# LayerNorm's mean and mean square in a one-core decoder layer: fp32 products against a column of ones, or fp32r products of split sums against a constant tile

## The chip, the cores and the metric

The kernel runs on one NeuronCore of one Trainium2 chip. The metric is the device time of one execution in microseconds, the median of several runs. A profile is one further execution with the hardware profiler on. All its times count from the first instruction of the span.

## The reference, cut to what matters

One layer for 288 tokens (256 of a prompt, 8 × 4 of a decoding batch), model width 2048, everything in fp32. The change lies in the convolution branch, in the `layernorm` line:

```
h = rmsnorm(x, norm1_g)
proj = h @ w_in + b_in
a, gate, z = proj[..., :D_CONV], proj[..., D_CONV:2 * D_CONV], proj[..., 2 * D_CONV:]
u = a * jax.nn.sigmoid(gate)
c = jax.nn.silu(layernorm(depthwise_causal_conv(u_ext, conv_w, conv_b), ln_g, ln_b))
p = multiscale_pool(z_ext, pos0) @ pool_w * pool_scale
x = x + jnp.concatenate([c, p], axis=-1) @ w_out
x = x + jnp.square(jax.nn.relu(rmsnorm(x, norm2_g) @ w_ff1)) @ w_ff2
return rmsnorm(x, norm_f)
```

`layernorm` takes mean and variance over the 1024 channels of the convolution, per token.

## The kernel before

**Layout.** Channels lie on the 128 partitions, the 288 tokens along the free axis. A product is 128 × 128 weights against 128 × 288 tokens in one PSUM bank. Each fp32 matrix product is made of three fp32r products of split operands, high × high, low × high, high × low. The activations are split once. The weights come from HBM in 512 KB halves (`wr`). ScalarE writes the high part (`whi`, L275); VectorE (`wlo`, L280), GpSimd (L283) or, in a few cases, a DMA that adds writes the low part. Five buffers of each kind circulate, so the cast of a later half waits until TensorE has read the last product from the buffer that it takes over.

**Order of the work.** `gemm` (L311) writes out the products of one pair of banks, in pairs of k tiles, 12 products per k pair and bank, with all weights of a half used before the next half. Its argument `between` names functions that are called at a given k; what they issue stands there on TensorE, and the products of the gemm that follow are issued after it. The rest of the order on each engine comes from a scheduler that goes by priorities (the order of the code; `later` moves code down by a number) and by its own estimates. Each engine works through its queue in order, so an instruction that waits holds up everything behind it.

**The stages around the change.** First the input projection and pooling run in the order of `SEQUENCE` (L45); the last three steps are the pooling products of group 1, convolution pair 7 and the pooling products of group 0 (`pp`, then `dx` on ScalarE at L510, VectorE at L511). Then eight gemms, called g = 0 to 7 here, multiply the pooled half `mixp` (tiles `dx`) with the lower half of `w_out`. While they run, VectorE finishes the depthwise convolution (L457), and LayerNorm's steps are placed between their products:

- `ln_mean` (L551), at k = 4 of g = 5: two fp32 products of the sums of `c` with `ones`, a 128 × 128 tile of 1/1024. Each shows as two records per product in the trace. `sum_c` holds the sum of seven of the eight channel groups, made on GpSimd; the eighth is the second half of `c`'s last tile.
- `ln_sums` (L556), at k = 6 of g = 6: VectorE subtracts the mean (L559), ScalarE squares (L561), VectorE adds (L565, L566). `rsqrt_sums` (L239) brings 288 sums onto 96 partitions × 3 with three small fp32 products (`pt<-ones,q`), ScalarE takes the root (L251) and loads the table for SiLU (L209), VectorE makes the inverse root by one Newton step (L254 to L257) on 96 × 3 numbers.
- `ln_rows` (L570), at k = 2 of g = 7: `spread` (L260) brings the 288 values back as a row on all 128 partitions, with three fp32 products (`pt<-ident,st`).

After the eight gemms comes the loop over `cs`, four tiles of two channel groups. VectorE multiplies by the row (L587), ScalarE applies SiLU twice (L590) and casts the high part (L592), VectorE makes the low part (L593). These tiles (`mx`) are the operands of the next eight gemms, with the upper half of `w_out`; the first two of them are interleaved on TensorE and begin with the first `mx` tile. Behind them follow the two feed-forward products, which take most of the time, and the last norm.

ScalarE's function tables: Sigmoid during the projections; a dummy activation `few` (L209) loads Sqrt right behind the last Sigmoid (L442, L443), and Silu behind the root (L251).

Second norm (L633): it already has the form that the change gives to LayerNorm, with a cast (L637), a subtraction (L638), two fp32r products with a constant tile, a root over 128 × 288 (L643) and `inverse_root` (L232) on 128 × 288.

Of the kernel before, what the change touches and what calls it, by code (L numbers as in the profile page):

```python
# [86 lines left out]
def trunk_kernel(ctx: ExitStack, tc: tile.TileContext, io):  # L87
# [139 lines left out]
    cst = const.tile([P, 32], F32, name="cst")  # L227
# [206 lines left out]
    def conv_pair(i, banks):  # L434
# [7 lines left out]
        if i == N8 - 1:  # L442
            load_table(AF.Sqrt, tg[:, 0:1])  # L443
# [105 lines left out]
    norm = {}  # L549

    def ln_mean():  # L551
        norm["mean"] = ms("pmean")[:, 0, :T]
        mm(norm["mean"], ones, sum_c[:, 0, :], start=True, stop=False)
        return mm(norm["mean"], ones, cs[-1][:, 1, :], start=False, stop=True)

    def ln_sums():  # L556
        ssc = None
        for c in cs:
            nc.vector.tensor_tensor(c, c, norm["mean"][:, None, :].to_broadcast([P, 2, T]), op=ALU.subtract)  # L559
            q = tmpp.tile([P, 2, T], F32, name=nm("q2"), tag="ag" if ssc is None else "ag2", bufs=2)  # L560
            nc.scalar.activation(q, c, AF.Square)  # L561
            if ssc is None:
                ssc = q
            else:
                nc.vector.tensor_tensor(ssc, ssc, q, op=ALU.add)  # L565
        nc.vector.tensor_tensor(ssc[:, 0, :], ssc[:, 0, :], ssc[:, 1, :], op=ALU.add)  # L566
# [18 lines left out]
    for j, c in enumerate(cs):  # L585
        n = tmpp.tile([P, 2, T], F32, name=nm("n"), tag="ag", bufs=2)
        nc.vector.tensor_tensor(n, c, norm["rows"][:, None, :].to_broadcast([P, 2, T]), op=ALU.mult)  # L587
        for m in range(2):
            i = 2 * j + m
            nc.scalar.activation(n[:, m, :], n[:, m, :], AF.Silu, bias=v("ln_b", i), scale=v("ln_g", i))  # L590
        mh, ml = act2("mx")
        nc.scalar.copy(mh, n)  # L592
        nc.vector.tensor_tensor(ml, n, f32(mh), op=ALU.subtract)  # L593
# [185 lines left out]
```

## Time and profile before

| | us |
|---|---|
| median of 3 runs | 1085.36 (1085.34 to 1086.2) |
| the profiled execution, its own time | 1084.97 |
| its span, first to last instruction | 1082.9 |
| TensorE busy in the span | 1071.1 (99%) |
| mean granted TensorE clock | 0.997 |

The profiled execution lies 0.39 us under the median, and 2.1 us of it lie outside the span. Busy time on TensorE counts overlapping products once, so 99% says that there are hardly any gaps, not that nothing could be gained: a product that is not needed is busy as well.

### The profile page before, as it was taken

Reading aid. Unit: us, or ns where it says so; the run is one execution under the profiler, and the core shown is the slowest. Engines: PE = TensorE matmul, PEld = TensorE weight load, DVE = VectorE, ACT = ScalarE, POOL = GpSimd, SP = SyncE. Lnnn points to the kernel's source line nnn. Section 1 sums busy time; section 2 is a strip of 40 time slices with the busy share of each in tenths; the row PEclk is TensorE's granted clock in tenths of the full one; section 3 lists DMA queues with packets and bytes.
Section 4 is the critical chain, followed back from the end, with each engine's and each line's share of the span. In section 5 each row is a group of like instructions: output and inputs, shape, how many; then the busy total and the mean of one; then the engine's idle time right before and its main releaser. Section 6 shows DMA issues by size and latency. Waiting matters only on the chain.

```text
span 1082.9 us, 19574 instructions
## 1 busy us (share of the span) xinstructions
PE 1071.1 (99%) x8198; PEld 1068.5 (99%) x8198; DVE 636.5 (59%) x817; ACT 477.4 (44%) x584; POOL 173.8 (16%) x180
## 2 busy tenths in 40 slices
PE   9999999999999999999999999999999999999996
PEld 8999999999999999999999999999999999999996
DVE  8899999678655544445544444545544445554552
ACT  8654455475544433334443333444433334444441
POOL 0878979512000000000000000000000000000001
PEclk9999999999999999999999999999999999999998
DMA  9896477545555555555555555555555555555522
GB/s 333 281 268 182 137 209 231 172 152 176 173 163 170 174 168 165 175 164 168 175 169 165 174 167 167 174 171 164 172 169 166 173 172 164 171 172 163 172 78 88
DMA packets 58696, 190.71 MB, mean 176 GB/s; under 512 B 6256, under 2 KB 12016, under 8 KB 58608
## 3 DMA queue, kind: packets, MB, share of 16 engines
q1 hardware_dynamic: 56336, 184.09, 53.0%
q0 software_dynamic: 1008, 3.67, 1.8%
q10 hardware_dynamic: 1264, 1.70, 0.5%
q8 instruction: 64, 1.05, 0.4%
q14 instruction: 24, 0.20, 0.1%
HBM read 185.16 MB, written 4.28 MB: 175 GB/s over the span
## 4 chain that ended last, share of the span: by engine, by line
PE 76%; issue 21%; ACT 1%; DMA 1%; DVE 1%; POOL 0%; SPq 0%; POOLq 0%; DVEq 0%
PE ac L306 75%; DMA wr<-in_w 1%; PE pp L306 0%; ACT whi L275 0%; DVE wlo L280 0%; POOL xT L715 0%; ACT n L590 0%; DVE z_all L414 0%; ACT L209 0%; ACT z_all L412 0%; PE pt L306 0%; PE pmean L306 0%; POOLq L765 0%; DVE xT L690 0%; DVE n L587 0%
## 5 line engine op out<-in xcount | busy, mean ns | idle before, releaser
L275 ACT CAST whi<-wr 128x1024 fp32r<-128x1024 f32 (+1 forms) x341 | 355.5, 1043 | 557.5 <-PE ac L306 536.0
L280 DVE TENSOR_TENSOR wlo<-wr,whi 128x1024 fp32r<-128x1024 f32 (+1 forms) x297 | 363.7, 1225 | 348.4 <-ACT whi L275 348.4
L306 PE MATMUL ac<-ax,whi 128*128 128x288 f32 x2048 | 351.1, 292 | 0.0
L306 PE MATMUL ac<-fx,whi 128*128 128x288 f32 x2048 | 350.2, 292 | 0.0
L306 PEld LDWEIGHTS ac<-ax,whi 128*128 128x128 f32 x2048 | 296.0, 187 | 0.0
L306 PEld LDWEIGHTS ac<-fx,whi 128*128 128x128 f32 x2048 | 295.7, 187 | 0.0
L306 PE MATMUL ac<-ax,wlo 128*128 128x288 f32 x1024 | 217.4, 292 | 0.0
L306 PE MATMUL ac<-fx,wlo 128*128 128x288 f32 x1024 | 216.4, 292 | 0.0
L306 PEld LDWEIGHTS ac<-ax,wlo 128*128 128x128 f32 x1024 | 162.6, 187 | 0.0
L306 PEld LDWEIGHTS ac<-fx,wlo 128*128 128x128 f32 x1024 | 162.3, 187 | 0.0
L306 PE MATMUL ac<-hx,whi 128*128 128x288 f32 x768 | 136.2, 293 | 0.7 <-DVE hx L361 0.3
L715 POOL TENSOR_TENSOR xT<-xT,rf 128x288 f32<-128x288 f32 x4 | 3.0, 792 | 800.1 <-ACT rf L719 800.1
L306 PEld LDWEIGHTS ac<-hx,whi 128*128 128x128 f32 x768 | 113.3, 188 | 1.4 <-ACT whi L275 0.9
L283 POOL TENSOR_TENSOR wlo<-wr,whi 128x512 fp32r<-128x512 f32 x74 | 100.6, 1415 | 35.4 <-ACT whi L275 34.4
L457 DVE SCALAR_TENSOR_TENSOR pc<-u_all,vec,pc 128x256 f32<-128x256 f32 x232 | 99.5, 483 | 1.9 <-ACT pc L454 0.7
L306 PE MATMUL ac<-hx,wlo 128*128 128x288 f32 x384 | 86.2, 293 | 0.3 <-DVE wlo L280 0.2
L306 PEld LDWEIGHTS ac<-hx,wlo 128*128 128x128 f32 x384 | 62.7, 188 | 0.7 <-DVE wlo L280 0.7
L306 PE MATMUL ac<-dx,whi 128*128 128x288 f32 x256 | 46.1, 296 | 0.3 <-ACT dx L510 0.3
L306 PE MATMUL ac<-mx,whi 128*128 128x288 f32 x256 | 45.2, 294 | 0.1
L659 DVE SCALAR_TENSOR_TENSOR t<-ac,r 128x576 f32<-128x576 f32 x32 | 24.2, 758 | 25.2 <-PE ac L306 25.2
L306 PEld LDWEIGHTS ac<-dx,whi 128*128 128x128 f32 x256 | 37.9, 188 | 0.7 <-ACT dx L510 0.6
L306 PEld LDWEIGHTS ac<-mx,whi 128*128 128x128 f32 x256 | 37.5, 188 | 0.6 <-ACT mx L592 0.3
(130 smaller groups left out, 515.0 us busy)
## 6 DMA issues: line engine op xcount, KB each, us to landing
wr<-in_w SPq DMA_DIRECT2D x335, 512.0 KB, 3.7
wlo<-in_w POOLq DMA_DIRECT2D x7, 512.0 KB, 8.5
xT<-in_xT SPq DMA_DIRECT2D x7, 288.0 KB, 7.1
out_u_out<-u_all SPq DMA_DIRECT2D x1, 1208.0 KB, 8.9
u_all<-in_hist_c SPq DMA_DIRECT2D x8, 136.0 KB, 5.6
wr<-in_w SPq DMA_DIRECT2D x4, 256.0 KB, 3.5
out_z_out<-z_all SPq DMA_DIRECT2D x1, 668.0 KB, 8.9
z_all<-in_hist_p SPq DMA_DIRECT2D x4, 152.0 KB, 7.7
```

What stands on the lines that cost most here:

```text
L275: nc.scalar.copy(hi, raw)
L280: nc.vector.tensor_tensor(lo, raw, f32(hi), op=ALU.subtract)
L283: nc.gpsimd.tensor_tensor(lo[:, j : j + 2, :], raw[:, j : j + 2, :], f32(hi[:, j : j + 2, :]), op=ALU.subtract)
L306: last = nc.tensor.matmul(*args, **kw)
L457: nc.vector.scalar_tensor_tensor(out=dst, in0=up[:, w : w + SEQ], scalar=cwv[:, w : w + 1], in1=pc, op0=ALU.mult, op1=ALU.add)
L659: nc.vector.scalar_tensor_tensor(out=t, in0=bk[:, :, :T], scalar=0.0, in1=both(rows2[0]), op0=ALU.max, op1=ALU.mult)
L715: eng.tensor_tensor(xk, xk, r[:, None, :].to_broadcast([P, n, T]), op=ALU.mult)
```

## The change

- The sums of `c` are split into high and low parts (tile `hm`, new lines 553 and 554): ScalarE casts, GpSimd or VectorE subtracts. `ln_mean` becomes four fp32r products with `means_c`, a new constant tile of 1/1024 that GpSimd makes at the start.
- In `ln_sums` the sum of squares is cast by ScalarE and subtracted by VectorE (tile `hs`), and two fp32r products with `means_c` put the mean square on all partitions. Root, table load and `inverse_root` follow on 128 × 288 numbers, the last three steps of it in PSUM. `rsqrt_sums` and `spread` are no longer called here, and `ln_rows` with its three products is gone.
- `ln_sums` and the loop over `cs` stand in `later(-LATER)`, at high priority.
- The load of the Sqrt table moves from the last Sigmoid to behind the last pooling products.

```diff
-        if i == N8 - 1:
-            load_table(AF.Sqrt, tg[:, 0:1])
...
+    load_table(AF.Sqrt, f32(mixp[1][0])[:, 0:1])
...
+    hm = actp.tile([P, 4, T], F32R, name="hm", tag="act")
+    for (hi, lo), part, eng in (((1, 0), sum_c[:, 0, :], nc.gpsimd), ((3, 2), cs[-1][:, 1, :], nc.vector)):
+        nc.scalar.copy(hm[:, hi, :], part)
+        eng.tensor_tensor(hm[:, lo, :], part, f32(hm[:, hi, :]), op=ALU.subtract)
+    def products(bank, parts):
+        for j, part in enumerate(parts):
+            last = mm(bank, means_c, part, start=j == 0, stop=j == len(parts) - 1)
+        return last
     def ln_mean():
         norm["mean"] = ms("pmean")[:, 0, :T]
-        mm(norm["mean"], ones, sum_c[:, 0, :], start=True, stop=False)
-        return mm(norm["mean"], ones, cs[-1][:, 1, :], start=False, stop=True)
+        return products(norm["mean"], [hm[:, j, :] for j in (1, 0, 3, 2)])
...
-        norm["sums"] = rsqrt_sums([ssc[:, 0, :]], 1.0 / DC, AF.Silu)
-        return norm["sums"][2]
-    def ln_rows():
-        norm["rows"], last = spread(norm["sums"])
+            hs = actp.tile([P, 4, T], F32R, name="hs", tag="act")
+            hi, lo = hs[:, 1, :], hs[:, 0, :]
+            nc.scalar.copy(hi, ssc[:, 0, :])
+            nc.vector.tensor_tensor(lo, ssc[:, 0, :], f32(hi), op=ALU.subtract)
+            bk, rl = ms("pt"), row("rl")
+            mean, root = bk[:, 0, :T], bk[:, 1, :T]
+            last = products(mean, [hi, lo])
+            nc.scalar.activation(root, mean, AF.Sqrt, bias=eps)
+            load_table(AF.Silu, root[:, 0:1])
+            inverse_root(mean, root, rl, root)
+            norm["rows"] = root
         return last
-    BETWEEN = {5: {4: ln_mean}, 6: {6: ln_sums}, 7: {2: ln_rows}}
+    BETWEEN = {5: {4: ln_mean}, 6: {6: ln_sums}}
...
     for j, c in enumerate(cs):
...
+        with later(-LATER):
```

How the order on the engines moves. In the changed kernel the line numbers from L229 to L441 are larger by 2 (casts stand at L277, low parts at L282), those from L444 to L546 are as before, and those behind the new code are larger by 17 or 18. Buffer numbers are larger by a few.

**Place 1: ScalarE at the end of the pooling products** (`tg` is the last Sigmoid, `dx` the last two pooling results). Before:

```order
L441 ACTIVATE tg_2193<-ac_2088,vec 128x288
L209 ACT_TABLE_LOAD
L209 ACTIVATE few<-tg_2193 128x1
L510 ACTIVATE dx_2040<-pp_2233,vec 128x288
L275 CAST whi_2386<-wr_2379 128x1024
L454 ACTIVATE pc_1717<-u_all,vec 128x256
L510 ACTIVATE dx_2040<-pp_2233,vec 128x288
L275 CAST whi_2445<-wr_2441 128x1024
```

The same place on ScalarE in the changed kernel:

```order
L443 ACTIVATE tg_2195<-ac_2090,vec 128x288
L510 ACTIVATE dx_2042<-pp_2234,vec 128x288
L277 CAST whi_2393<-wr_2386 128x1024
L454 ACTIVATE pc_1719<-u_all,vec 128x256
L510 ACTIVATE dx_2042<-pp_2234,vec 128x288
L209 ACT_TABLE_LOAD
L209 ACTIVATE few<-dx_2042 128x1
L277 CAST whi_2452<-wr_2448 128x1024
```

The load and its dummy activation have moved behind both `dx`.

**Place 2: VectorE from the end of the squares' sum** (q at 128x288 is its last addition) **to the multiplication by the row**. Before:

```order
L566 TENSOR_TENSOR q_2689<-q_2689 128x288
L280 TENSOR_TENSOR wlo_2804<-wr_2797,whi_2803 128x1024
L250 TENSOR_SCALAR st_2708<-pt_2704 96x3
L254 RECIPROCAL st_2708<-st_2708 96x3
L255 TENSOR_TENSOR st_2708<-st_2708 96x3
L256 SCALAR_TENSOR_TENSOR st_2708<-st_2708 96x3
L257 SCALAR_TENSOR_TENSOR st_2708<-st_2708 96x3
L582 TENSOR_TENSOR xT<-xT,ac_2651 128x576
L280 TENSOR_TENSOR wlo_2891<-wr_2886,whi_2890 128x1024
L587 TENSOR_TENSOR n_2808<-c_637,pt_2704 128x576
L587 TENSOR_TENSOR n_2815<-c_721,pt_2704 128x576
```

The same place on VectorE in the changed kernel:

```order
L577 TENSOR_TENSOR q_2698<-q_2698 128x288
L282 TENSOR_TENSOR wlo_2811<-wr_2804,whi_2810 128x1024
L581 TENSOR_TENSOR hs<-q_2698,hs 128x288
L236 RECIPROCAL rl_2717<-pt_2716 128x288
L599 TENSOR_TENSOR xT<-xT,ac_2660 128x576
L282 TENSOR_TENSOR wlo_2898<-wr_2893,whi_2897 128x1024
L237 SCALAR_TENSOR_TENSOR pt_2716<-pt_2716,rl_2717 128x288
L238 SCALAR_TENSOR_TENSOR pt_2716<-pt_2716,rl_2717 128x288
L239 SCALAR_TENSOR_TENSOR pt_2716<-pt_2716,rl_2717 128x288
L282 TENSOR_TENSOR wlo_2902<-wr_2895,whi_2901 128x1024
L605 TENSOR_TENSOR n_2815<-c_639,pt_2716 128x576
L605 TENSOR_TENSOR n_2822<-c_723,pt_2716 128x576
```

The subtraction for `hs` now stands where TensorE's small result was fetched, behind a low part of weights (`wlo_2811`) that itself waits for a cast; one more low part (`wlo_2902`) has come ahead of the first `n`.

**Place 3: ScalarE from the root to the first `mx` tiles.** Before:

```order
L275 CAST whi_2803<-wr_2797 128x1024
L251 ACTIVATE st_2708<-st_2708 96x3
L209 ACT_TABLE_LOAD
L209 ACTIVATE few<-st_2708 96x1
L275 CAST whi_2890<-wr_2886 128x1024
L590 ACTIVATE n_2808<-n_2808,vec 128x288 x2
L275 CAST whi_2894<-wr_2888 128x1024
L590 ACTIVATE n_2815<-n_2815,vec 128x288 x2
L592 CAST mx_2812<-n_2808 128x576
L592 CAST mx_2819<-n_2815 128x576
L275 CAST whi_2961<-wr_2957 128x1024
```

The same place on ScalarE in the changed kernel:

```order
L277 CAST whi_2810<-wr_2804 128x1024
L580 CAST hs<-q_2698 128x288
L585 ACTIVATE pt_2716<-pt_2716,cst 128x288
L209 ACT_TABLE_LOAD
L209 ACTIVATE few<-pt_2716 128x1
L277 CAST whi_2897<-wr_2893 128x1024
L277 CAST whi_2901<-wr_2895 128x1024
L277 CAST whi_2968<-wr_2964 128x1024
L608 ACTIVATE n_2815<-n_2815,vec 128x288 x2
L608 ACTIVATE n_2822<-n_2822,vec 128x288 x2
L610 CAST mx_2819<-n_2815 128x576
L610 CAST mx_2826<-n_2822 128x576
```

Three weight casts now stand ahead of the first SiLU, where there was one; the third, `whi_2968`, takes over the buffer that g = 7 reads to its end (before, its counterpart `whi_2961` stood behind the two `mx` casts). On TensorE the new products stand where the old ones stood; the order of SyncE's and GpSimd's DMAs is unchanged.

More of the change, by code (lines that the diff above doesn't have):

```diff
@@ L226, in trunk_kernel @@
     nc.vector.tensor_scalar(means, ones, DC / D, None, op0=ALU.mult)
-    cst = const.tile([P, 32], F32, name="cst")
+    means_c = const.tile([P, P], F32R, name="means_c")
+    nc.gpsimd.tensor_scalar(means_c, ones, 1.0, None, op0=ALU.mult)
+    cst = const.tile([P, 48], F32, name="cst")
     eps, mean_d = cst[:, 0:1], cst[:, 1:2]
@@ L585, in trunk_kernel @@
     for j, c in enumerate(cs):
[L586 to L593, printed above, removed]
+        with later(-LATER):
+            n = tmpp.tile([P, 2, T], F32, name=nm("n"), tag="ag", bufs=2)
+            nc.vector.tensor_tensor(n, c, norm["rows"][:, None, :].to_broadcast([P, 2, T]), op=ALU.mult)
+            for m in range(2):
+                i = 2 * j + m
+                nc.scalar.activation(n[:, m, :], n[:, m, :], AF.Silu, bias=v("ln_b", i), scale=v("ln_g", i))
+            mh, ml = act2("mx")
+            nc.scalar.copy(mh, n)
+            nc.vector.tensor_tensor(ml, n, f32(mh), op=ALU.subtract)
         mixc += halves((mh, ml))
```

20 lines of the change are left out of this document (10 added, 10 removed).

## The prediction

> **What bounds the kernel now.** I read the page first, then TensorE's timeline at the four places that the change touches, then ScalarE's and VectorE's at the same times.
>
> ```profile
> PE 1071.1 (99%) x8198; PEld 1068.5 (99%) x8198; DVE 636.5 (59%) x817; ACT 477.4 (44%) x584; POOL 173.8 (16%) x180
> ```
>
> TensorE is the bound nearly everywhere: 1071.1 us over 8198 records is 0.131 us for each product. So the change can only be worth what it takes from or adds to TensorE's queue, in products or in gaps. The rows below begin with the start in us and the time to the end of the last of the xN merged products; a gap shows as starts further apart than 0.131 us per product.
>
> The Sqrt table load, on TensorE and on ScalarE:
>
> ```profile
> 169.09 0.43 PE L306 MATMUL pp<-dx,whi 128*128 128x288 f32 x2
> ...
> 170.16 0.43 PE L306 MATMUL ac<-dx,whi 128*128 128x288 f32 x2
> 170.94 0.66 PE L306 MATMUL ac<-dx,whi 128*128 128x288 f32 x3 [0.34 <-ACT dx L510]
> 171.43 0.43 PE L306 MATMUL ac<-dx,wlo 128*128 128x288 f32 x2
> ```
>
> ```profile
> 169.00 1.28 ACT L209 ACT_TABLE_LOAD   x1
> 170.40 0.48 ACT L510 ACTIVATE dx<-pp,vec 128x288 fp32r<-128x288 f32 x1
> ```
>
> Five products from 170.16 take 171.43 - 170.16 = 1.27 us, where 0.66 would do: a gap of 0.61 us. TensorE waits for `dx`, which stands behind the load on ScalarE.
>
> LayerNorm's three groups of small products:
>
> ```profile
> 200.94 0.65 PE L306 MATMUL pmean<-sum_c,ones 128*128 128x288 f32 x2
> 201.43 0.65 PE L306 MATMUL pmean<-c,ones 128*128 128x288 f32 x2
> 201.70 0.65 PE L306 MATMUL ac<-dx,whi 128*128 128x288 f32 x2
> 202.18 0.43 PE L306 MATMUL ac<-dx,wlo 128*128 128x288 f32 x2
> ```
>
> ```profile
> 209.91 0.59 PE L306 MATMUL pt<-ones,q 128*96 128x1 f32 x6
> 210.36 0.52 PE L306 MATMUL ac<-dx,whi 128*128 128x288 f32 x2
> 210.71 0.42 PE L306 MATMUL ac<-dx,wlo 128*128 128x288 f32 x2
> 213.62 0.80 PE L306 MATMUL pt<-ident,st 96*128 96x96 f32 x6
> 214.21 0.51 PE L306 MATMUL ac<-dx,whi 128*128 128x288 f32 x2
> 214.56 0.43 PE L306 MATMUL ac<-dx,wlo 128*128 128x288 f32 x2
> ```
>
> From each group's start to the second row behind it, less the two ordinary products between (0.26 us): the mean costs 1.24 - 0.26 = 0.98 us of the queue, the sums 0.80 - 0.26 = 0.54, the row 0.94 - 0.26 = 0.68.
>
> The first `mx` products:
>
> ```profile
> 218.80 0.43 PE L306 MATMUL ac<-dx,whi 128*128 128x288 f32 x2
> 219.33 0.53 PE L306 MATMUL ac<-mx,whi 128*128 128x288 f32 x2
> 219.70 0.43 PE L306 MATMUL ac<-mx,wlo 128*128 128x288 f32 x2
> 220.08 0.53 PE L306 MATMUL ac<-mx,whi 128*128 128x288 f32 x2
> 220.44 0.42 PE L306 MATMUL ac<-mx,wlo 128*128 128x288 f32 x2
> 220.75 0.80 PE L306 MATMUL ac<-mx,whi 128*128 128x288 f32 x4
> 221.38 0.42 PE L306 MATMUL ac<-mx,wlo 128*128 128x288 f32 x2
> ```
>
> Fourteen products take 2.58 us instead of 1.83: gaps of 0.75 us in all. A product behind a gap is followed 0.11 us late (0.37 for the pair at 219.33, instead of 0.26). I call that the restart.
>
> **What the change takes away.** Behind the moved load, `dx` starts when the last pooling products (`pp`) are done, at 169.09 + 0.43 = 169.52, and ends 0.48 us later, at 170.0, ahead of TensorE's arrival at 170.16 + 0.26 = 170.42. Were it late, the gap would come back in part. The gap of **0.61** goes; the load then lies in front of casts that wait for TensorE anyway. Four fp32r products for the mean: 0.52 instead of 0.98, **0.45** saved (the second norm's fp32r products with a constant tile have the 0.29 us of any other). So TensorE is 1.06 us early from 202 us on, and so are the mean's users on VectorE and ScalarE, which wait for it. Two products for the squares instead of 0.54: **0.28** saved. The row's **0.68** is gone.
>
> **What it adds at no cost.** The casts and subtractions for `hm`, and `means_c`.
>
> ```profile
> 26.97 3.95 POOL L283 TENSOR_TENSOR wlo<-wr,whi 128x512 fp32r<-128x512 f32 x2 [24.65 <-ACT whi L275]
> 202.40 2.56 POOL L283 TENSOR_TENSOR wlo<-wr,whi 128x512 fp32r<-128x512 f32 x2 [0.72 <-ACT whi L275]
> ```
>
> GpSimd makes `means_c` in 24.65 us of idle time at the start. Its `hm` subtraction (about 0.7 us, as a pass over 512 columns takes 1.28 here) delays two pairs of low parts; the idle 0.72 us takes most of it up, and these low parts end at 205 and are used by g = 7 from 212 on. Uncovered it would be 0.7 us; I take nothing. The short casts on ScalarE and the subtraction on VectorE stand in front of instructions that wait for TensorE. No DMA changes its place on SyncE or GpSimd.
>
> **What it adds on the path, first: the product of the squares.** Place 2 of the order shows the new subtraction for `hs` behind `wlo`, which waits for a cast.
>
> ```profile
> 208.55 1.05 ACT L275 CAST whi<-wr 128x1024 fp32r<-128x1024 f32 x1 [1.60 <-issue]
> ```
>
> ```profile
> 208.74 0.46 DVE L566 TENSOR_TENSOR q<-q 128x288 f32<-128x288 f32 x1
> 209.64 1.23 DVE L280 TENSOR_TENSOR wlo<-wr,whi 128x1024 fp32r<-128x1024 f32 x1 [0.44 <-ACT whi L275]
> 210.78 0.15 DVE L250 TENSOR_SCALAR st<-pt 96x3 f32<-96x3 f32 x1
> 219.27 0.76 DVE L582 TENSOR_TENSOR xT<-xT,ac 128x576 f32<-128x576 f32 x1 [0.34 <-PE ac L306]
> ```
>
> ```profile
> L638 DVE TENSOR_TENSOR hl<-ss,hl x1: 451/451/451, 275.7 to 275.7; 128x288 fp32r<-128x288 f32 x1
> L643 ACT ACTIVATE mean<-mean,cst x1: 476/476/476, 285.2 to 285.2; 128x288 f32<-128x288 f32 x1
> L234 DVE RECIPROCAL r<-mean x1: 1958/1958/1958, 285.7 to 285.7; 128x288 f32<-128x288 f32 x1
> ```
>
> That cast is released by the fourth k tile of g = 6, so it moves 1.06 us earlier with TensorE. VectorE is free at 210.78 - 1.06 = 209.72, subtracts for 0.45 (the row of the same step in the second norm) and ends at 210.17; the second product starts at 210.22. TensorE could have started it at 209.91 - 1.06 + 0.13 = 208.98. The wait is 1.24 us, with the restart **1.35**. Bounds: nothing, were the subtraction ahead of `wlo`; 1.5, were the cast for `hs` late too. TensorE goes on at 210.46, where the old kernel went on at 210.45: all that was won up to here is given back.
>
> **Second: the first `mx` tile.** TensorE ends g = 7 0.68 us earlier than before; the next product's turn is at 219.06 - 0.68 + 0.01 = 218.39, the last product's end 0.16 later, at 218.55. Two chains lead to the first SiLU.
>
> VectorE's: the product ends at 210.62; root 0.48 to 211.14; table load 1.28 and the dummy activation 0.2 to 212.63. The reciprocal's wait on ScalarE counts up to the dummy activation, so it starts at 212.67 and takes 1.96 on 288 columns, to 214.63. Behind it stand in place 2, each less 0.08 of overlap: addition 0.67, low part 1.15, three steps of about 0.48 (0.45 as in L638's row, and a little for each waiting for the one before), low part 1.15, and `n` 0.75, so `n` ends at 214.55 + 0.67 + 1.15 + 1.45 + 1.15 + 0.75 = 219.72. ScalarE's: the third cast of place 3 waits for the end of g = 7, so the SiLU cannot start before 218.6 + 0.95 = 219.55. The later one holds: 219.76.
>
> ```profile
> 217.57 1.15 ACT L590 ACTIVATE n<-n,vec 128x288 f32<-128x288 f32 x2
> 218.62 1.23 ACT L592 CAST mx<-n 128x576 fp32r<-128x576 f32 x2
> ```
>
> Four SiLUs now go ahead of the first cast: twice 1.05. From the cast's start to TensorE's start it was 219.33 - 218.62 = 0.71. So `mx` is used from 219.76 + 2.10 + 0.71 = 222.57: a wait of 4.18, with the restart 4.29, instead of gaps of 0.75: **3.54** more. The second tile's cast comes 0.6 us after the first. The third stands behind four more SiLUs, whose `n` VectorE makes behind the first two low parts, 4.6 us behind the first; TensorE has 44 products, 5.8 us, ahead of it. So no further gap. Bounds: 3.2 (reciprocal not held by the dummy, overlaps a little larger) to 4.2 (each wait 0.1 us longer).
>
> **Sum.** -0.61 - 0.45 - 0.28 + 1.35 - 0.68 + 3.54 = **+2.87** us. From the profiled execution's 1084.97 that is 1087.8; its median is 0.39 higher, so **1088.2**, with 1087.4 to 1088.9 from the bounds of the two waits. A measurement of this kernel can tell 0.2% from no change, 2.17 us: 1083.2 and 1087.5 are the bounds.
>
> **Rivals.**
>
> *The clock falls in the long wait.* The tail shows what an idle TensorE does to its clock (columns of the stretches: length, then busy us of each engine, then the granted clock).
>
> ```profile
> 1072.99 0.83 PE L707 MATMUL again<-ident,cst 96*128 96x96 f32 x6
> ```
>
> ```profile
> 1074.01:1077.42 3.41, 0.00 (x0) 0.00 (x0) 3.25 (x4) 0.24 (x1) 3.04 (x4) 1.00 0.82 304
> 1077.43:1079.00 1.57, 0.00 (x0) 0.00 (x0) 0.00 (x0) 0.00 (x0) 0.00 (x0) 0.50 1.05 402
> 1.04 4.21 PE L215 MATMUL warm<-ones 128*128 128x128 f32 x18 [1.04 <-DVE cst L230]
> ```
>
> The last product ended at 1073.82, and at 1077.43, 3.6 us later, the clock was halved. My wait is idle from 218.55 to 222.57, 4.0 us. Counted from the last product it would halve every time; judged in fixed stretches of up to 3.6 us, an idle of 4.0 covers a whole one in (4.0 - 3.6) / 3.6 = 11% of the executions. I give 0.17 together. If the slow clock lasts as long as the first, slow-spaced products of the start, 4.2 us, half of it is lost: 2.1 us more, 1090.3. The Trainium skill, in "TensorE: Matmul & The Clock Gate", section "Part 1: The HAM clock gate", has free-running windows of 3413 ns, one idle window halving the clock. By that rule the share is (4.0 - 3.4) / 3.4 = 17% and the price about 1.7 us, 1089.9; the tail's 3.6 us agrees with it.
>
> *Only one wait is new.* If the squares' subtraction is ready by 208.98, everything behind is 1.35 us earlier: +1.5, 1086.9. For it: the sum of squares itself (L566) is ready at 209.20 - 1.06 = 208.14, 0.7 us before TensorE's turn. Against: place 2. Chance 0.11.
>
> *Faster: the first `mx` is not late.* If the first SiLU starts by 218.39 - 2.81 = 215.58, which is when it started before, neither wait shows: -0.61 - 0.45 - 0.28 - 0.68 - 0.75 = -2.8, 1082.6. The high priority speaks for it; the place of the third cast, which cannot run before 218.6, and the 1.96 of the reciprocal speak against. Chance 0.06.
>
> **How the numbers follow.** Forecast 0.66, slow clock 0.17, one wait 0.11, faster 0.06. The range takes in the forecast's own bounds, the slow clock and most of the third case: 1086.8 to 1090.4. Of the forecast's 0.66 a tenth ends under 1087.5, so slower has 0.60 + 0.17 = 0.77, the same 0.11 + 0.06 = 0.17, faster 0.06.
>
> **What would show it.** Right: no gap at `dx`; `pmean` four records 0.13 apart; a wait of 1.2 us at the second `pt` product, on VectorE's `hs`; no `ident` products; a wait of 4 us at the first `mx`, on ScalarE, with the third cast right behind g = 7; an unchanged rest. Wrong: `hs` before 209, a SiLU start before 219, new gaps behind 223, or a clock under 1.00 there.

## The result, and the profile after

The changed kernel takes 1095.81 us (median of 4 runs, 1092.57 to 1096.44) beside 1085.35 (1085.31 to 1086.2): a ratio of 1.0091, with an interval of 1.0078 to 1.0103. It is slower, by 10.5 us where +2.9 was forecast, and outside the range. The profiled execution took 1096.19, its span 1094.4 instead of 1082.9: 11.5 us to account for.

```profile
PE 1073.8 (98%) x8188; PEld 1071.3 (98%) x8188; DVE 646.8 (59%) x818; ACT 480.4 (44%) x587; POOL 174.6 (16%) x182
...
PE ac L308 75%; DMA wr<-in_w 1%; DVE hm L554 1%; PE pp L308 1%; ACT whi L277 0%; DVE pc L457 0%; DVE wlo L282 0%; POOL xT L733 0%; ACT n L608 0%; DVE z_all L416 0%; PE pt L308 0%; ACT z_all L414 0%; POOLq L783 0%; DVE xT L708 0%; DVE xT L599 0%
```

TensorE has ten records less and is busy 2.7 us longer: some products became slow. In the chain of waits one VectorE instruction, `hm`, holds 1% of the span by itself.

TensorE's timeline after, at the four places that the prediction quotes of before:

```profile
169.81 0.43 PE L308 MATMUL pp<-dx,whi 128*128 128x288 f32 x2
...
170.88 0.97 PE L308 MATMUL ac<-dx,whi 128*128 128x288 f32 x5
171.69 0.42 PE L308 MATMUL ac<-dx,wlo 128*128 128x288 f32 x2
...
201.18 0.55 PE L308 MATMUL pmean<-hm,means_c 128*128 128x288 f32 x3
205.60 0.40 PE L308 MATMUL pmean<-hm,means_c 128*128 128x288 f32 x1 [3.87 <-DVE hm L554]
205.84 0.42 PE L308 MATMUL ac<-dx,whi 128*128 128x288 f32 x2
206.10 0.42 PE L308 MATMUL ac<-dx,wlo 128*128 128x288 f32 x2
...
215.43 0.40 PE L308 MATMUL pt<-hs,means_c 128*128 128x288 f32 x1
216.72 0.40 PE L308 MATMUL pt<-hs,means_c 128*128 128x288 f32 x1 [0.90 <-DVE hs L581]
...
224.68 0.43 PE L308 MATMUL ac<-dx,whi 128*128 128x288 f32 x2
228.90 0.85 PE L308 MATMUL ac<-mx,whi 128*128 128x288 f32 x2 [3.79 <-ACT mx L610]
```

The gap at `dx` is gone but for 0.15 us. The waits at `pt` and `mx` are where the prediction put them. The wait at the fourth `pmean` product is new. Setting each row's start against its counterpart of before divides the 11.5 us:

| stretch | from | worked out | us |
|---|---|---|---|
| up to the last pooling products | start of the kernel | 169.81 - 169.09 | +0.72 |
| the table load | `dx` | (201.18 - 200.94) - 0.72 | -0.48 |
| the mean | `pmean` | (206.10 - 201.18) - (202.18 - 200.94) | +3.68 |
| squares, row, and slow products | to the end of g = 7 | (224.68 - 218.80) - (206.10 - 202.18) | +1.96 |
| first `mx` | the wait | (228.90 - 219.33) - (224.68 - 218.80) | +3.69 |
| behind it | slow products | 11.5 - (228.90 - 219.33) | +1.93 |

The first line has to do with no instruction that moved in the three places. In this profile a weight tile of the first products landed later, which its cast shows (9.23 us here, 8.57 before). That doesn't settle it: in hm_gpsimd below the cast is at 8.63, and the last pooling products come 0.83 us late all the same. All eight profiles with the new sum of squares are 0.4 to 1.2 us late there; table_only is 0.2 early and table_mean 0.1 late. With one profile of each kernel it stays open whether the change costs this.

```profile
9.23 1.05 ACT L277 CAST whi<-wr 128x1024 fp32r<-128x1024 f32 x1 [0.34 <-DMA wr<-in_w]
```

VectorE and GpSimd beside the wait at `pmean`, the first of GpSimd's rows being the last one with idle time ahead of it:

```profile
196.81 8.73 DVE L554 TENSOR_TENSOR hm<-c,hm 128x288 fp32r<-128x288 f32 x1 [0.50 <-ACT hm L553]
...
216.22 0.45 DVE L581 TENSOR_TENSOR hs<-q,hs 128x288 fp32r<-128x288 f32 x1
```

```profile
164.51 8.09 POOL L285 TENSOR_TENSOR wlo<-wr,whi 128x512 fp32r<-128x512 f32 x6 [1.75 <-ACT whi L277]
...
196.97 0.86 POOL L554 TENSOR_TENSOR hm<-sum_c,hm 128x288 fp32r<-128x288 f32 x1
197.74 7.50 POOL L285 TENSOR_TENSOR wlo<-wr,whi 128x512 fp32r<-128x512 f32 x6
```

The same instruction, 128 x 288 from two SBUF inputs, takes 0.45 us at 216 with GpSimd idle and 8.73 at 196.81. It ends at 205.54, where GpSimd's row of passes ends at 205.24. GpSimd shows no idle time between 164.51 and that end. Of before, the most that a VectorE instruction lost beside GpSimd was 1.1 us (minimum, median and maximum in ns behind the xN):

```profile
L280 DVE TENSOR_TENSOR wlo<-wr,whi x297: 679/1226/2310, 5.3 to 1054.9; 128x1024 fp32r<-128x1024 f32 x146, 128x512 fp32r<-128x512 f32 x3
```

The granted clock behind the two long waits (columns of the stretches: length; busy us and instructions of TensorE, weight loads, VectorE, ScalarE, GpSimd; granted clock; share and rate of the DMAs):

```profile
203.34:206.75 3.41, 1.15 (x8) 1.15 (x9) 3.41 (x3) 0.00 (x0) 1.89 (x2) 1.00 0.60 207
206.80:210.10 3.30, 3.30 (x15) 3.30 (x15) 2.74 (x5) 2.03 (x3) 0.00 (x0) 0.50 0.34 123
223.90:227.20 3.30, 1.21 (x10) 0.97 (x8) 3.30 (x5) 2.06 (x4) 0.00 (x0) 1.00 0.61 214
227.30:230.60 3.30, 1.70 (x7) 1.70 (x8) 2.90 (x5) 2.12 (x4) 0.00 (x0) 0.50 0.49 153
230.70:234.00 3.30, 3.30 (x16) 3.30 (x15) 1.08 (x3) 2.93 (x6) 0.00 (x0) 0.50 0.21 81
234.10:237.40 3.30, 3.30 (x26) 3.30 (x26) 1.73 (x3) 1.35 (x2) 0.00 (x0) 1.00 0.00 0
```

A slow stretch holds 15 or 16 products where a full one holds 26. One stretch behind `pmean` and two behind `mx` are slow: some 11 x 0.131 = 1.4 us, and about 2 us, which is what the table has beyond the predicted terms (+1.96 instead of +0.39, and the last line).

### The profile page after: what moved, and what is told of

It is laid out like the page before. It is cut to its first block, busy times and chain, and to the rows that moved or that the text cites. A ratio compares the mean times of both kernels' runs of the same rounds, so it can differ in the third digit from the quotient of the medians.

```text
span 1094.4 us, 19558 instructions
## 1 busy us (share of the span) xinstructions
PE 1073.8 (98%) x8188; PEld 1071.3 (98%) x8188; DVE 646.8 (59%) x818; ACT 480.4 (44%) x587; POOL 174.6 (16%) x182
## 4 chain that ended last, share of the span: by engine, by line
PE 76%; issue 20%; DVE 2%; DMA 1%; ACT 1%; POOL 0%; POOLq 0%; DVEq 0%
PE ac L308 75%; DMA wr<-in_w 1%; DVE hm L554 1%; PE pp L308 1%; ACT whi L277 0%; DVE pc L457 0%; DVE wlo L282 0%; POOL xT L733 0%; ACT n L608 0%; DVE z_all L416 0%; PE pt L308 0%; ACT z_all L414 0%; POOLq L783 0%; DVE xT L708 0%; DVE xT L599 0%
## 5 line engine op out<-in xcount | busy, mean ns | idle before, releaser
L277 ACT CAST whi<-wr 128x1024 fp32r<-128x1024 f32 (+1 forms) x341 | 356.4, 1046 | 562.2 <-PE ac L308 537.0
L282 DVE TENSOR_TENSOR wlo<-wr,whi 128x1024 fp32r<-128x1024 f32 (+1 forms) x297 | 363.6, 1225 | 347.6 <-ACT whi L277 347.5
```

What stands on the lines that cost most here:

```text
L277: nc.scalar.copy(hi, raw)
L282: nc.vector.tensor_tensor(lo, raw, f32(hi), op=ALU.subtract)
```

## Experiments

Two questions: what held VectorE's `hm` for 8 us, and what the slow clock follows. Theory A is that GpSimd's passes hold up a VectorE instruction with two SBUF inputs; theory B that another cause does.

**hm_psum: one of VectorE's inputs in PSUM.**

```
...
+            norm["bank"] = ms("pmean")
+            nc.scalar.copy(norm["bank"][:, 1, :T], high)
+            high = norm["bank"][:, 1, :T]
...
-        eng.tensor_tensor(hm[:, lo, :], part, f32(hm[:, hi, :]), op=ALU.subtract)
+        eng.tensor_tensor(hm[:, lo, :], part, high, op=ALU.subtract)
...
```

> The changed kernel with one edit: ScalarE copies the high part of the last channel group's sums once more, into PSUM, and VectorE subtracts that copy, so its subtraction has one input in SBUF instead of two. Same values, same place in VectorE's queue, 0.4 us more on ScalarE. Theory A (VectorE's subtraction with both inputs in SBUF is held off as long as GpSimd runs its low-part passes, 197.0 to 205.2 us): the subtraction takes 0.45 to 0.5 us and ends before 199, the fourth pmean product follows the third by 0.13 us, the wait of 4.16 us and the halved clock behind it are gone; the waits at the second pt product (1.3 us) and at the first mx product (about 4 us) stay. Time: 1088.0 without a halving of the clock in the mx wait, 1089.8 to 1090.3 with one. Theory B (something else held it: the cast of its input, the write of an fp32r tile that GpSimd writes too, or a wait that the trace does not show): it still ends at 205 and the time stays at 1093 to 1096.

Measured: 1090.39 us (1089.18 to 1090.91), ratio 1.0044 (1.0031 to 1.0057). VectorE, TensorE and the clock in its trace:

```profile
197.29 0.45 DVE L559 TENSOR_TENSOR hm<-c,pmean 128x288 fp32r<-128x288 f32 x1 [0.94 <-ACT pmean L557]
```

```profile
201.23 0.68 PE L308 MATMUL pmean<-hm,means_c 128*128 128x288 f32 x4
...
223.36 0.85 PE L308 MATMUL ac<-mx,whi 128*128 128x288 f32 x2 [3.78 <-ACT mx L615]
```

```profile
219.10:222.40 3.30, 0.48 (x4) 0.25 (x2) 3.30 (x5) 2.78 (x5) 0.00 (x0) 1.00 0.69 246
222.50:225.80 3.30, 2.44 (x10) 2.44 (x11) 2.92 (x5) 1.65 (x4) 0.00 (x0) 0.50 0.52 164
```

0.45 us, beside the same row of GpSimd's; four `pmean` products in a row; no slow clock there. Theory B falls. The `mx` wait and the slow clock behind it stay, and the time is 0.44% above before.

**hm_gpsimd: GpSimd makes both low parts.** Edit: `nc.vector` becomes `nc.gpsimd` in the list of parts.

> The changed kernel with one edit: GpSimd, not VectorE, subtracts for both low parts of hm; the second stands in its queue behind one half tile of weights (two passes). Theory A (VectorE held off by GpSimd's passes): no VectorE instruction with two SBUF inputs stands there any more; GpSimd's two subtractions take 0.86 us each, the second ends at about 201.1, just ahead of the fourth pmean product's turn at 201.6, so the 4.16 us wait is gone or below 0.3 us; 1088 to 1090.5, as with one input in PSUM. Theory B (the input c or its cast is late, or the tile itself is the matter): the second subtraction is late on GpSimd too and the wait stays near 4 us, 1093 to 1096.

Measured: 1090.67 us (1089.57 to 1092.39), ratio 1.005 (1.0034 to 1.0065). The four products again follow each other (201.28, x4); the median lies just above theory A's 1088 to 1090.5. A second VectorE instruction is now held up, the first addition of squares:

```profile
204.67 2.15 DVE L576 TENSOR_TENSOR q<-q,q 128x576 f32<-128x576 f32 x1
```

2.15 us instead of 0.75, and `hs` comes 0.8 us later than in hm_psum. Moving work from VectorE to GpSimd moves the victim.

**mean_fp32: the mean as it was, the rest of the change.** Edit: no `hm`; `ln_mean` issues its two fp32 products with `ones`.

> The changed kernel with the mean put back: two fp32 products of the sums with the fp32 constant tile, no hm. The rest of the change stays (table load later, squares as two fp32r products, no spread row, high priority). This is what the prediction's sum was about without its two terms on the mean. Theory A: no wait at pmean, the mean costs 0.98 us again instead of 0.52, everything else as predicted: 1088.2 + 0.45 = 1088.65 where the clock holds in the mx wait, about 1.7 to 2.3 us more, 1090.4 to 1091, where it is halved. Theory B (the mean's form is not what cost time, the high priority or the squares are): 1093 to 1096.

Measured: 1089.72 us (1089.65 to 1091.21), ratio 1.0043 (1.0031 to 1.0056). It lies between theory A's two figures (1088.65 with the clock held, 1090.4 to 1091 with it halved, as it was in this profile), and far from theory B's. By the ratios, 1.0091 and 1.0043, the new form of the mean costs 5.2 us.

**table_only and table_mean: the parts that should gain.** The first moves only the load; the second adds the fp32r mean with one input in PSUM.

```
-        if i == N8 - 1:
-            load_table(AF.Sqrt, tg[:, 0:1])
...
+    load_table(AF.Sqrt, f32(mixp[1][0])[:, 0:1])
```

> The kernel before with the Sqrt table load alone moved behind the last pooling products. By the prediction's first term the gap of 0.61 us at the dx products goes and nothing else changes: ratio 0.9994, 1084.75 beside 1085.36. The rival, that the gap is given back at the next thing that is late (LayerNorm's chain ends with the first mx products, which wait for TensorE's own products only in part): 0.2 us or less remains of it.

> The kernel before with the two parts that should gain: the Sqrt table load moved, and the mean as four fp32r products of split sums with the constant tile, VectorE's subtraction with one input in PSUM. Sum of squares, spread row and the rest as before. By the prediction's terms -0.61 - 0.45 = -1.06 us: 1084.3 beside 1085.4, ratio 0.9990, no new wait. The rival: the casts and subtractions for the split, or the earlier chain behind the mean, delay the weights' low parts, or the gain of the mean is given back at the first mx products: 1084.7 to 1085.4.

Measured: 1084.58 us (1084.2 to 1085.23) beside 1085.72, ratio 0.999 (0.9982 to 0.9999); and 1084.07 (1083.72 to 1085.91) beside 1085.21, ratio 0.9991 (0.9982 to 1.0). Both gains are there in the traces: the gap at `dx` is down to some 0.15 us, and the four `pmean` products take 0.53 us. The medians are 1.14 us lower in each, where -0.61 and -1.06 were forecast. That is at the edge of what these runs can tell from nothing, and the mean's own part can't be told by them. The second has the lowest median of all kernels here.

**warm: hm_psum, with TensorE kept busy in the mx wait.**

```
...
+    for j in range(26):
+        with tc.issue_after(hold if j == 0 else hold.ins):
+            hold = nc.tensor.matmul(idle1[:, :T], means_c, norm["hi"], start=True, stop=True)
...
```

> The kernel with one VectorE input in PSUM (hm_psum), and 26 products that nobody reads behind the last product of the eight gemms, on TensorE in the wait for the first mx tile: 26 x 0.131 = 3.4 us of the 4.07 us wait, so that the first mx product starts when it did. Theory A (a wait of 4 us costs more than itself, since the granted clock is halved behind it for one or two stretches of 3.41 us, 1.55 to 2.7 us in the profiles so far): the granted clock stays at 1.00 there, the products behind are 0.131 apart, and the time falls by 1.5 to 2.7 us against hm_psum, to 1088.0 to 1088.9, which is also the prediction's sum without its rival. Theory B (the products behind the wait are slow for another reason, such as weights or the second mx tile being late): nothing changes, or it gets slower by what the added products delay.

Measured: 1087.94 us (1087.54 to 1089.26), ratio 1.0026 (1.0015 to 1.0037).

```profile
219.38 3.63 PE L624 MATMUL idle<-hs,means_c 128*128 128x288 f32 x26
223.34 0.54 PE L308 MATMUL ac<-mx,whi 128*128 128x288 f32 x2 [0.33 <-ACT mx L616]
```

```profile
223.20:226.40 3.20, 3.06 (x23) 3.06 (x24) 2.76 (x4) 1.56 (x4) 0.00 (x0) 1.00 0.51 166
```

The first `mx` product starts when it did in hm_psum (223.36), and the clock stays at 1.00: 2.0 us less against before (1.0044 - 1.0026 of 1085) for 26 products that nobody reads. With both surprises taken away, the median is 2.73 us above before; the prediction's sum was +2.87. The interval reaches from 1.6 to 4.0 us.

**no_newton: the chain to the first mx made shorter.** hm_psum without the three steps behind the reciprocal (`nc.vector.reciprocal(root, root)` in place of `inverse_root`).

> hm_psum without the three steps of the inverse root behind the reciprocal of LayerNorm (left out, so the row is less exact). The order changes with it in one place: ScalarE's third weight cast stands behind the first mx cast instead of in front of the SiLUs. Theory A (VectorE's chain over 288 numbers and the cast in front of the SiLUs end at about the same time and set the mx wait together): the chain is 1.45 us shorter and the cast out of the way, so the first mx product comes 1.4 to 1.5 us earlier and the wait is about 2.6 us instead of 4.07. A wait that short may leave the clock at 1.00 in part of the executions: 1086.5 to 1088.9. Theory B (the mx wait is set by something else, such as the SiLU table or the c tiles): the wait stays at 4 us, 1089 to 1091.

Measured: 1085.52 us (1084.38 to 1086.18), ratio 1.0003 (0.9993 to 1.0012).

```profile
218.77 0.43 PE L308 MATMUL ac<-dx,whi 128*128 128x288 f32 x2
220.48 0.53 PE L308 MATMUL ac<-mx,whi 128*128 128x288 f32 x2 [1.29 <-ACT mx L615]
```

The wait falls by 2.5 us, more than the 1.45 of the steps, and the time lies below the 1086.5 us that was expected at least. Two more instructions have moved: VectorE's second low part, 1.22 us, now stands behind `n`, and ScalarE's third cast, which waits for the end of g = 7, behind the first `mx` cast instead of ahead of the SiLUs. In the changed kernel VectorE and ScalarE reach the first SiLU together:

```profile
225.27 1.41 DVE L605 TENSOR_TENSOR n<-c,pt 128x576 f32<-128x576 f32 x2
```

```profile
225.14 1.05 ACT L277 CAST whi<-wr 128x1024 fp32r<-128x1024 f32 x1 [2.09 <-PE ac L308]
226.09 2.19 ACT L608 ACTIVATE n<-n,vec 128x288 f32<-128x288 f32 x4
```

The first of the two `n` ends at 226.02 and the cast at 226.19. So no_newton takes both away at once, and what either would be worth alone is not shown. What is left of the wait, 1.45 us, leaves the clock alone, and the change breaks even (the row is less exact then).

**ports_clock: both effects by themselves.**

> A measurement by itself; the layer is left out and the outputs are zeros. First part: VectorE subtracts 128 x 288 numbers beside GpSimd's subtractions of 128 x 512 (1.25 us each), started by the same ScalarE instruction. Two inputs in SBUF beside 1, 3 and 6 passes; one input in PSUM beside 6; one input and a constant beside 6; five subtractions with two inputs in SBUF beside 6. Theory A (held off as long as GpSimd works without a break): about 1.3, 3.9 and 7.6 us, against 0.45 with one input in PSUM; the five together end 2 us behind the last pass. Theory A2 (held off only by the pass that is running): 1.3 us beside 3 and 6 passes too. Theory B (no such thing): 0.45 us everywhere. Second part: trains of 84 to 96 products with idle stretches of six lengths between them, some 1.6 to 3.8 us, eight of each, at varied places in the 3.41 us raster in which the granted clock changes. Theory A (a stretch of the raster that is mostly idle halves the clock in the next one; from the profiles so far 58% idle does and 49% doesn't): idle stretches below 1.7 us never halve it, those above 3.8 always, and between them the idle share of the fuller stretch decides. Theory B (only a stretch that is idle from end to end halves it): none of these idle lengths below 3.4 us ever halves it.

First part, VectorE's subtractions (L127 beside 1, 3 and 6 passes; L129 with one input in PSUM; L131 with a constant; L134 five in a row):

```profile
13.64 0.45 DVE L127 TENSOR_TENSOR low<-part,high 128x288 f32<-128x288 f32 x1
16.31 1.36 DVE L127 TENSOR_TENSOR low<-part,high 128x288 f32<-128x288 f32 x1 [2.23 <-ACT part L123]
21.71 1.35 DVE L127 TENSOR_TENSOR low<-part,high 128x288 f32<-128x288 f32 x1 [4.04 <-ACT part L123]
30.77 0.46 DVE L129 TENSOR_TENSOR low<-part,high_p 128x288 f32<-128x288 f32 x1 [7.70 <-ACT part L123]
39.62 1.21 DVE L131 TENSOR_SCALAR low<-part 128x288 f32<-128x288 f32 x1 [8.39 <-ACT part L123]
48.52 7.09 DVE L134 TENSOR_TENSOR low<-part,high 128x288 f32<-128x288 f32 x5 [7.70 <-ACT part L123]
```

A pass is one of GpSimd's subtractions of 128 x 512. Beside 3 and 6 passes the subtraction takes 1.35 us, not 3.9 and 7.6: theory A as I had it, held up as long as GpSimd works, is wrong here, and A2 right. (The single pass was over at 13.63, before the first one came.) The 8.73 us needed more.

Second part: 47 idle stretches of TensorE. From the end of one product to the start of the next, as the profile has them, those of 1.9 us halved the clock in 1 of 8, of 2.4 in 3 of 8, of 2.8 in 8 of 8, of 3.2 in 4 of 8, of 3.6 in 7 of 8, of 4.0 in 7 of 7. The order is odd until they are laid on the raster of 3.41 us at which the clock changes. An idle stretch of 1.9 us that fell into one raster stretch, and one of 3.2 that was cut in the middle:

```profile
367.38:370.78 3.40, 1.47 (x11) 1.24 (x10) 1.77 (x3) 0.00 (x0) 0.00 (x0) 1.00 0.00 0
370.80:374.20 3.40, 3.40 (x17) 3.40 (x16) 0.00 (x0) 0.00 (x0) 0.00 (x0) 0.50 0.00 0
...
411.75:415.14 3.39, 1.90 (x15) 1.66 (x13) 1.42 (x2) 0.00 (x0) 0.00 (x0) 1.00 0.00 0
415.16:418.56 3.40, 1.72 (x13) 1.73 (x14) 1.59 (x2) 0.00 (x0) 0.00 (x0) 1.00 0.00 0
418.58:421.97 3.39, 3.39 (x28) 3.39 (x28) 0.00 (x0) 0.00 (x0) 0.00 (x0) 1.00 0.02 5
```

The first of them is idle for 1.93 / 3.41 = 0.57 of its length, the other two for 0.44 and 0.49. Over all of them, every raster stretch at full clock that was idle for 0.555 or more of its length was followed by a halved one (30 of 30), and none with 0.552 or less was. A halved stretch that was itself idle for 0.19 or more was followed by another (7 of 7); one with 0.17 or less was not. The kernels' own traces fit in: full-speed stretches idle for 0.57 (mean_fp32) and more were followed by a halved one, those idle for 0.50 (hm_shift) and less were not. So theory B, a whole idle stretch, falls. The `mx` wait is idle for 3.79 us, and where two raster stretches share it, one of them is idle for at least 3.79 / 2 / 3.41 = 0.556 of its length: it halves the clock nearly wherever it lies.

**hm_shift and ports_phase: the moment of arrival.** hm_shift puts one instruction in front of VectorE's subtraction; ports_phase varies the arrival by itself.

```
...
+            eng.tensor_scalar(norm["bank"][:, 1, :T], f32(hm[:, hi, :]), 1.0, None, op0=ALU.mult)
...
```

> The changed kernel with one short VectorE instruction (288 numbers from SBUF into PSUM, about 0.36 us) in front of the subtraction for hm, so that this arrives some 0.4 us later; it still has both inputs in SBUF and the same GpSimd passes beside it. In the changed kernel it arrived at 196.81, 0.26 us ahead of the end of a GpSimd pass, and was held off for seven passes; in the measurement by itself each one that arrived 0.2 us into a pass waited for the rest of that pass only. Theory A3 (one that arrives early in a pass gets its turn when that pass ends; one that arrives in the last 0.3 us is passed over, and goes on being so until GpSimd has a break): the subtraction arrives about 0.1 to 0.2 us into the next pass, takes 1.0 to 1.3 us, and the wait at pmean is gone: 1089 to 1091. Theory A (held off as long as GpSimd works without a break, whenever it arrives): again 8 us, 1093 to 1096.5. Theory A2 (only ever held off by the pass that runs; the 8.73 us had another cause): 1089 to 1091 too, told apart from A3 by the other measurement.

> A measurement by itself; the layer is left out and the outputs are zeros. 54 times, six GpSimd subtractions (128 x 512, fp32r out, 1.25 us each, 7.5 us without a break) start with a ScalarE instruction, and one VectorE subtraction of 128 x 288 with two inputs in SBUF (fp32r out, output and second input in one tile as in the kernel) comes 27 different times later, 0.09 us apart, over two passes; in the first half each GpSimd pass is waited for by ScalarE, in the second only the last one. Theory A3 (passed over for all the passes that follow where it arrives in the last 0.3 us of a pass): durations fall from about 1.5 to about 0.7 us as it arrives later in a pass, and some three or four arrivals before each of the two pass ends show 4 to 8 us. Theory A2 (only the running pass holds it off): 0.45 to 1.7 us everywhere, in a sawtooth. A dependence on who waits for the passes would show as a difference between the halves.

Measured: hm_shift 1094.03 us (1091.66, 1092.28, 1095.78, 1096.48), ratio 1.0092 (1.0072 to 1.0111). The profile is of the run with 1091.66. There the subtraction arrived 0.2 us into one of GpSimd's instructions and was passed over all the same, for four more:

```profile
197.11 0.46 DVE L556 TENSOR_SCALAR pmean<-hm 128x288 f32<-128x288 f32 x1 [0.50 <-ACT hm L553]
197.48 5.88 DVE L557 TENSOR_TENSOR hm<-c,hm 128x288 fp32r<-128x288 f32 x1
```

In ports_phase all 54 subtractions took 0.45 to 1.50 us, the rest of the running pass and their own 0.45, in a clean sawtooth; both halves alike. Theory A3 (the moment) falls with both, and A2 (the running pass alone) with hm_shift. What hm_shift and the changed kernel have in common, and ports_phase hasn't, is GpSimd's long row without a break.

**ports_long and ports_turns: the length of GpSimd's row.**

> A measurement by itself; the layer is left out and the outputs are zeros. GpSimd makes 10 to 38 subtractions of 128 x 512 without a break (1.22 to 1.25 us each), and one VectorE subtraction of 128 x 288 with two inputs in SBUF arrives after about 2, 6, 12, 18, 24 or 30 of them, with some eight still to come; three arrival phases each. A seventh form lets GpSimd pause for ScalarE after 24 passes and sends the VectorE subtraction behind the pause. In the changed kernel GpSimd had worked without a break for 32 us (some 27 passes) when VectorE's subtraction came and was passed over at seven pass ends; after at most two passes, in the measurement with varied arrival, none was passed over. Theory D (passes that follow each other for long run into each other: their records overlap by 0.04 us at first and by 0.10 us after 20 passes in the changed kernel, so that a pass end no longer lets VectorE in): after 2 passes at most 1.7 us as before, after 18 to 30 several us, and behind the pause at most 1.7 us again. Theory E (nothing that builds up; the seven missed turns have a cause that only the full kernel has, such as its weight transfers or TensorE's reads): at most 1.7 us everywhere.

> A measurement by itself; the layer is left out and the outputs are zeros. As the last one, with the arrival of VectorE's subtraction put right: after 8, 11, 13, 15, 17, 20, 24 and 30 unbroken GpSimd passes (with seven to come), two phases each. So far it was passed over by none after 1 to 10 passes and by all those left to come (2, 2 and 1) after 18, 18 and 19. Two more blocks send a subtraction after 6, 12, 18 and 24 passes of one row of 31. Theory D: up to some number between 10 and 18 it waits for the running pass only, at most 1.7 us, and from there on it is passed over for several or all of the seven passes, up to 9 us; where one had its turn every six passes, all four wait for one pass only, since each turn starts the count again. Theory F (no build-up: from a certain time on GpSimd's share of turns is by chance): long and short waits are mixed among all counts, and the second or later of the four is long as often as not.

In ports_long, arrivals in passes 1 to 10 waited for one pass at most, and those in passes 18, 18 and 19 took 3.57, 2.95 and 2.34 us, until the row was over; those meant for 18, 24 and 30 passes came at the row's end or behind it and tell nothing, and the pause after 24 was followed by 0.50 to 1.10. In ports_turns VectorE's subtraction arrived in pass 9, 12 or 14, and in 16, 18, 21, 25 or 31; here those in 14 and 16:

```profile
74.64 1.35 DVE L147 TENSOR_TENSOR act<-part,act 128x288 fp32r<-128x288 f32 x1
...
103.77 8.53 DVE L147 TENSOR_TENSOR act<-part,act 128x288 fp32r<-128x288 f32 x1
```

Up to pass 14, 0.74 to 1.35 us in 6 of 6. From pass 16 on, 7.92 to 8.59 us in 10 of 10: all passes that were left. Two rows of 31 had a VectorE subtraction in passes 7, 13, 19 and 25; the first and the last of one:

```profile
278.80 1.44 DVE L147 TENSOR_TENSOR act<-part,act 128x288 fp32r<-128x288 f32 x1
...
301.44 1.41 DVE L147 TENSOR_TENSOR act<-part,act 128x288 fp32r<-128x288 f32 x1
```

Never more than 1.44 in 8 of 8: each turn starts the count again. Theory D's count holds, E and F fall. The overlap of the passes' records, which I had taken for its sign, stayed at 0.04 us here, so that part of D is not the mechanism.

**hm_pause: a break in GpSimd's row, in the kernel itself.**

```
...
+    pause = nc.gpsimd.tensor_scalar(cst[:, 40:41], f32(hm[:, 2, 0:1]), 1.0, None, op0=ALU.mult)
+    with tc.issue_after(pause.ins):
+        nc.gpsimd.tensor_tensor(hm[:, 0, :], sum_c[:, 0, :], f32(hm[:, 1, :]), op=ALU.subtract)
```

> The changed kernel with a pause for GpSimd: one number that VectorE's subtraction for hm has written is copied by GpSimd ahead of its own subtraction for hm, which stands behind six passes now, so GpSimd stops at about 199.6 us until VectorE is done. VectorE's subtraction keeps both inputs in SBUF and arrives at 196.8 as in the changed kernel, behind some 27 passes without a break. Theory D (after a long unbroken row of passes the pass ends let nothing in, a break does): it waits until GpSimd stops and ends at 200.0 at the latest, 3.2 us long instead of 8.73 (less if it is let in at an earlier pass end); GpSimd's own part is ready at 201.1, the wait of 4.16 us at pmean is gone or below 0.3 us, time 1088.5 to 1091. Theory E (a cause that has nothing to do with GpSimd's row of passes): the subtraction takes as long as before, 6 to 9 us, and GpSimd waits for it: 1093 to 1097.

Measured: 1089.84 us (1089.66 to 1090.53), ratio 1.004 (1.0026 to 1.0054).

```profile
196.53 3.01 DVE L554 TENSOR_TENSOR hm<-c,hm 128x288 fp32r<-128x288 f32 x1 [0.50 <-ACT hm L553]
```

```profile
192.89 6.33 POOL L285 TENSOR_TENSOR wlo<-wr,whi 128x512 fp32r<-128x512 f32 x5
199.63 0.22 POOL L555 TENSOR_SCALAR cst<-hm 128x1 f32<-128x1 f32 x1 [0.41 <-DVE hm L554]
```

VectorE is let in when GpSimd stops at 199.2, and the wait at `pmean` is gone.

## Why the prediction was wrong, step by step

- **The step that failed: "The short casts on ScalarE and the subtraction on VectorE stand in front of instructions that wait for TensorE", at no cost.** The place was right: between the arrival at 197 us and the mean's users at 202, VectorE had 0.75 us of other work. The duration was not. I gave this subtraction no time at all (the like one for `hs` got 0.45 us, from a row of the second norm where GpSimd is idle), and looked at the queue and not at what ran beside it. It came during GpSimd's 25th instruction since VectorE's last turn beside it (`dx` at 165 us), and took 8.73 us. In the sum it stood as nothing; it cost 4.1 us at `pmean`, and 1.4 of slow products behind it. hm_psum, hm_gpsimd, mean_fp32 and hm_pause each remove it in another way. The trace of before had the warning in small, in the maximum of L280's row.
- **The rival "the clock falls in the long wait", at 0.17, came true in every profile with that wait.** The price was right: 2.1 us forecast, about 2 in the changed kernel, 2.0 between warm and hm_psum. The chance was wrong, because I asked for a whole stretch of the raster without work, and 0.555 of it was enough in ports_clock. The Trainium skill, in "TensorE: Matmul & The Clock Gate", section "Part 1: The HAM clock gate", states free-running windows of 3413 ns and half the clock behind an idle one. The traces agree on the raster; an idle window is one that is idle for 0.555 or more here.
- **Table load, -0.61:** -0.48; 0.15 us of the gap is left at the same place. By itself -1.1 us in the medians, which holds both 0.5 and 0.6 in its interval (-1.95 to -0.1).
- **Mean, -0.45:** four products in 0.53 us (table_mean) where two took 0.98. Right.
- **Squares, row and the wait at `pt`, -0.28 - 0.68 + 1.35 = +0.39:** +1.96 less 1.4 of slow products, 0.5. In hm_psum, without slow products there, it is 0.5 as well. VectorE's `hs` did stand behind `wlo`, and the second product started 1.29 us after the first, 1.16 late, where 1.24 was forecast. Right.
- **First `mx`, +3.54:** the wait was 228.90 - 224.68 less two products, 3.95 us, where 4.18 was forecast; what it adds, 3.69 less some 0.4 for the small gaps of before behind the first product, comes to 3.3. ScalarE's third cast did stand right behind g = 7, and the SiLUs behind it. Right in the main: the forecast has VectorE's chain end 0.2 us behind ScalarE's, and in the trace the two end together, the cast 0.17 us behind `n`. How much of the wait either causes alone isn't shown.
- **"The high priority speaks for" the faster case:** it does nothing. Without `later(-LATER)` every engine's order is the same row for row.
- The other terms sum to what was forecast: warm, which removes the two surprises, is at +2.73 us for +2.87. That it is so close is in part luck: the terms above are off by 0.1 to 0.2 us each, in both directions. In warm's profile the span is 3.6 us longer than before, 0.74 of it at the start.

Open: why the border lies at the fifteenth or sixteenth pass (the fifteenth was not tried), whether passes count or time (the arrivals in pass 14 came up to 16.6 us into the row, those in pass 16 from 18.7 us on), and why hm_shift's subtraction was let in before the row's end. Of the changed kernel's four runs one is 3 us below the others; hm_shift's fall into two groups 4 us apart. That VectorE is let in earlier in some executions is likely, and was only argued. Also open is the start, 0.7 us later in this profile.

## What to carry to other kernels

A VectorE instruction's duration belongs to what runs beside it: before giving GpSimd a long row of work, see which VectorE instructions with two SBUF inputs fall into it, and put one operand in PSUM or a break into the row. A TensorE wait of more than about 2 us can cost a half-speed stretch on top, and one of 4 did in every case here; unread products in the wait are the cheap remedy. And a shorter chain of products can buy a longer chain of everything else: here 1 us of products (the sums and the row) was saved for a chain over 288 numbers and an order of casts that made TensorE wait for 4.

## What the hardware showed

- VectorE beside GpSimd's subtractions of 128 x 512: two SBUF inputs 0.45 us plus the rest of the running pass (0.45 to 1.50 in 54 cases), one input in PSUM 0.46, a constant and SBUF to SBUF 1.21. The Trainium skill, in "SBUF — State Buffer", section "SBUF: two separate sides", states that of a VectorE instruction with two SBUF inputs and a GpSimd instruction that reads SBUF, whichever starts first gets a shared pair of ports for its whole instruction and the other is blocked. The sawtooth of ports_phase agrees.
- From the sixteenth pass of an unbroken row on, VectorE was no longer let in between the passes in ports_turns: 7.9 to 8.6 us in 10 of 10. A turn of VectorE's (1.44 us at most in 8 of 8) and a break (0.50 to 1.10 in 3 of 3) started the count again. In hm_shift's profile it was let in after four more passes, with the row going on.
- The clock is set in a raster of 3.41 us: in ports_clock it was halved behind every stretch idle for 0.555 of it or more, and restored behind every one idle for 0.17 or less.
